# Seven products in place of eight for the second pair of chunks in each feed-forward of a decoder trunk

## The chip, the core and the metric

The kernel runs on one core of a Trainium2 chip. The core has four engines that compute and that run their own instruction queues side by side: TensorE (PE; its weight loads are listed as PEld), VectorE (DVE), ScalarE (ACT) and GpSimd (POOL). SyncE (SP) only issues transfers. TensorE multiplies a stationary tile, which is loaded first, with a moving tile, and writes into PSUM, which has eight banks of 128 partitions x 512 float32; everything else lives in SBUF. Transfers (DMA) run on 16 engines that all queues share: SP's queue loads weights, POOL's queue carries the transfers that add what they bring to what lies at the destination.

The metric is the device time of one execution in microseconds (us), as a median over runs.

## The reference

Two layers, each of them a feed-forward, a mixer and another feed-forward, with a residual and a layer norm behind each of the six. 512 tokens, D_MODEL = 1024, D_FF = 2816, all in float32:

```python
def layer_norm(x, g, b):
    mu = jnp.mean(x, axis=-1, keepdims=True)
    var = jnp.mean(jnp.square(x - mu), axis=-1, keepdims=True)
    return (x - mu) * lax.rsqrt(var + LN_EPS) * g + b

def swiglu_ffn(x, w_gu, w_down):           # w_gu 1024 x 5632, w_down 2816 x 1024
    a, u = jnp.split(x @ w_gu, 2, axis=-1)
    return (jax.nn.silu(a) * u) @ w_down

for l in range(2):
    x = layer_norm(alpha * x + 0.5 * swiglu_ffn(x, ffn1_w_gu[l], ffn1_w_down[l]), ln1_g[l], ln1_b[l])
    x = layer_norm(alpha * x + hybrid_mixer(x, ...), ln2_g[l], ln2_b[l])
    x = layer_norm(alpha * x + 0.5 * swiglu_ffn(x, ffn2_w_gu[l], ffn2_w_down[l]), ln3_g[l], ln3_b[l])
```

The mixer (windowed attention and retention between two projections) is not touched by the change. What follows is about `x @ w_gu`, the up and gate product, in the four feed-forwards; they are called the first to the fourth, in order of time.

## The kernel before, in words

*Precision.* A float32 operand is held as two tiles of a reduced type: the high part is a rounding copy on ScalarE (L173), the low part is the difference between the operand and its high part, on DVE (L174). Such a pair is made by `split`. A product of two operands is three matmuls that add up in PSUM (`mm3`: high x high L188, high x low L189, low x high L190). The names are xh and xl for the activations, transposed, uh and ul for a weight unit of 128 x 1024, Th and Tl for combinations of the activations, raw for the weights as they come from memory.

*The layer's input.* The norm leaves each tile of 128 tokens in Y. Four transposes on TensorE (L488) fill one bank; the split then makes xh and xl from that bank, 512 columns at a time, two banks to a tile of tokens. Tokens 0 to 255 are there before the feed-forward's first matmul; the transposes of tokens 256 to 511 are put into the middle of its opening (`self.finish(self.pend[2:])`), on the schedule of the program text: it is the program's order that decides, and the scheduler keeps matmuls in that order.

*Pairs.* The 5632 columns of `w_gu` are taken in 11 pairs of chunks: a block of 256 columns of a and the 256 columns of u that belong to it. A pair is computed in one of two ways.

- Plain (pairs 0 and 1): four weight units (two of a, two of u), each multiplied with all tokens. For pair 0 the tokens are taken in two halves, so that the work on tokens 0 to 255 goes on while the others are not there yet; one product of pair 1 is drawn forward behind each half of pair 0.
- Strassen's form in the variant of Winograd (pairs 2 to 10, the list `SEVEN`): for a and for u seven half-sized products in place of eight, so 14 products of 12 matmuls of 256 columns. `seven_items` prepares seven weight units: two of them plain blocks, one made of the two lower right blocks, four from sums of blocks (S, at L321, L322, L325, L326, on DVE). `glu7` multiplies. In it the first four products need plain blocks of xh and xl for tokens 0 to 255 only; the others need combinations of the activations T1 to T4 or the block for tokens 256 to 511. The partial results are copied out of PSUM into Q and added to there on DVE. For the combinations, `sums_of_x` first rebuilds x = xh + xl in four additions on DVE (L556), into the part of hT that is written last, and then makes four differences (L560), each split into Th and Tl.

hT is the result of the pair, silu(a) x u x 0.5, written at L631 by DVE (or by the gate of a plain pair).

*The short row of repeated matmuls.* Before the first Strassen pair four matmuls run whose result is thrown away (`lead`, L460: the bank is started afresh by the next matmul).

*Weights.* `Weights` hands out units in the order of its items. It looks LOOK = 6 units ahead, at most UBUFS = 6 units and two raw buffers of 1 MB are in use, and a load is issued (SP's queue, L181) when a raw buffer comes free. The sums, the casts and the low parts of the coming units stand on DVE and ScalarE between the work on results.

*The down projection* at the end of each feed-forward uses the same form; there POOL's queue adds weight blocks from memory onto R (L394).

*Tasks.* `spawn` gives a generator a time in steps; `step`, called after each product, runs those that are due, and `finish` runs the rest.

Of the kernel before, what the change touches and what calls it, by code (L numbers as in the profile page):

```python
# [7 lines left out]
F32 = mybir.dt.float32  # L8
# [25 lines left out]
SEVEN = (2, 3, 4, 5, 6, 7, 8, 9, 10)  # L34
# [65 lines left out]
class Trunk:  # L100
    def __init__(self, tc, ctx):
# [6 lines left out]
        self.pace = None  # L108
        self.halves = 2
# [238 lines left out]
    def ffn_items(self, gu, down, key):  # L348
        items = []
        for fp in range(NFP):  # L350
            a = self.cols_item(gu, fp * 256, (key, "a", fp))
            u = self.cols_item(gu, DFF + fp * 256, (key, "u", fp))
            if fp == 0:
                items += [a[0], u[0], a[1], u[1]]
            else:
                items += self.seven_items(a, u) if fp in SEVEN else a + u
# [99 lines left out]
    def lead(self, out, u):  # L456

        for _ in range(4):
# [23 lines left out]
    def to_xT(self, src, t, c0, dst=None):  # L482
# [8 lines left out]
        self.split(xh[:, c0 : c0 + 4, ts], xl[:, c0 : c0 + 4, ts], bv)  # L491

    def y_to_xT(self, t):
        self.to_xT(self.Y[:, t, :512], t, 0)
        self.to_xT(self.Y[:, t, 512:], t, 4)
# [40 lines left out]
    def ffn(self, g_, b, out=None):  # L536
        nc, tc, W = self.nc, self.tc, self.W
        with ExitStack() as ctx:
# [8 lines left out]

            def sums_of_x():

                x = hT[:, NF - KC :, :]  # L550
                B = [[x[:, i * H : (i + 1) * H, j * 256 : (j + 1) * 256] for j in range(2)] for i in range(2)]
# [26 lines left out]
            def glu7(fp):  # L578
# [4 lines left out]
                for m in range(2):  # L583
# [4 lines left out]
                    if fp == SEVEN[0] and m == 0:  # L588
# [6 lines left out]
                    nc.vector.tensor_add(Q[m][:, 0], Q[m][:, 0], B[m][:, :256])  # L595
                us = W.get()
                u22 = W.get()
                for m in range(2):
                    C.append(self.ps())
                    u = W.get() if m else us  # L600
                    product(A[m], u, 1, T2, False)
                    nc.scalar.copy(Q[m][:, 1], A[m][:, :256])
                    product(C[m], u, 0, T1)
# [599 lines left out]
```

## Time and profile before

| | |
|---|---|
| median of 3 runs | 1752.91 us (1752.52 to 1752.96) |
| the profiled execution | 1752.16 us, with a span of 1750.4 us in the trace |
| granted TensorE clock, mean | 0.999 |
| busy: PE, DVE, ACT, POOL | 1739.2, 1415.5, 927.6, 182.7 us |

An instruction's row gives its start in us, its duration, its engine, its line in the kernel, the operation with result <- operands, and in brackets the idle time of its engine ahead of it with what ended it. "128x1024" is partitions x elements. In a view of windows, "x113" behind a busy time is a number of instructions, and PEclk is the granted clock as a share of full speed. In the queues' view a transfer's row is followed by the time from issue to landing. In the chain of waits a name with q, as PEq, is an engine's sequencer.

### The profile page before, as it was taken

What the parts mean: (1) busy time and instruction counts of PE and PEld (TensorE: products, weight loads), DVE (VectorE), ACT (ScalarE), POOL (GpSimd) and SP (SyncE); (2) the same over time, 40 slices, a digit from 0 to 9 for tenths busy, and PEclk for the clock granted to TensorE, in tenths of its full rate; (3) what the DMA queues carried; (4) which work ended last, traced back from release to release, by engine and by line L of the source; (5) the groups of instructions that cost most, each with busy time, mean ns of one, the idle gap of its engine ahead of it and who ended that gap; (6) DMA issues with size and microseconds to landing.
All of it is one profiled execution on the core that took longest, in us unless ns stands there. A gap on an engine that the chain in (4) does not pass through costs nothing.

```text
span 1750.4 us, 29200 instructions
## 1 busy us (share of the span) xinstructions
PE 1739.2 (99%) x11946; PEld 1580.1 (90%) x11946; DVE 1415.5 (81%) x1975; ACT 927.6 (53%) x1456; POOL 182.7 (10%) x154
## 2 busy tenths in 40 slices
PE   9999999999999999999999999999999999999998
PEld 9999988887789999998899999889877899999886
DVE  7888888856757889879898988988567587988887
ACT  5455656378712455555435556554785234555551
POOL 0000032111111000014000000312011110000231
PEclk9999999999999999999999999999999999999999
DMA  6234389323222243279423334982233123334891
GB/s 193 97 108 134 126 214 220 98 86 95 73 74 73 74 141 101 97 219 217 130 67 109 115 97 157 219 190 91 92 89 97 49 91 103 98 98 144 209 212 48
DMA packets 163765, 216.34 MB, mean 124 GB/s; under 512 B 5168, under 2 KB 116528, under 8 KB 163632
## 3 DMA queue, kind: packets, MB, share of 16 engines
q1 hardware_dynamic: 141872, 172.55, 30.5%
q0 software_dynamic: 21760, 41.95, 13.2%
q8 instruction: 93, 1.52, 0.4%
q14 instruction: 40, 0.33, 0.1%
HBM read 212.38 MB, written 2.10 MB: 123 GB/s over the span
## 4 chain that ended last, share of the span: by engine, by line
PE 48%; DVE 2%; DMA 0%; issue 0%; ACT 0%; POOLq 0%; DVEq 0%; ACTq 0%
PE ps L188 15%; PE ps L189 15%; PE ps L190 15%; PE ps L488 0%; DMA raw<-in_ffn_w_gu_dram 0%; PE ps L1030 0%; PE ps L995 0%; PE ps L1082 0%; PE ps L1022 0%; DVE Y L522 0%; PE ps L1044 0%; DVE ul L174 0%; DVE st L515 0%; DVE Y L513 0%; DVE xl L174 0%; DVE Y L525 0%
## 5 line engine op out<-in xcount | busy, mean ns | idle before, releaser
L188 PE MATMUL ps<-xh,uh 128*128 128x256 f32 (+1 forms) x1616 | 476.0, 295 | 0.0
L189 PE MATMUL ps<-xl,uh 128*128 128x256 f32 (+1 forms) x1616 | 473.0, 293 | 0.5 <-DVE xl L174 0.4
L190 PE MATMUL ps<-xh,ul 128*128 128x256 f32 (+1 forms) x1616 | 473.1, 293 | 0.4 <-DVE ul L174 0.4
L173 ACT CAST uh<-raw 128x1024 fp32r<-128x1024 f32 (+1 forms) x274 | 236.6, 884 | 233.3 <-PE ps L189 127.7
L174 DVE TENSOR_TENSOR ul<-raw,uh 128x1024 fp32r<-128x1024 f32 (+1 forms) x274 | 273.6, 1014 | 56.8 <-ACT uh L173 56.4
L188 PE MATMUL ps<-Th,uh 128*128 128x256 f32 x1152 | 318.0, 276 | 0.0
L189 PE MATMUL ps<-Tl,uh 128*128 128x256 f32 x1152 | 318.0, 276 | 0.0
L190 PE MATMUL ps<-Th,ul 128*128 128x256 f32 x1152 | 318.0, 276 | 0.0
L188 PEld LDWEIGHTS ps<-xh,uh 128*128 128x128 f32 x1616 | 304.1, 188 | 10.5 <-issue 1.6
L190 PEld LDWEIGHTS ps<-xh,ul 128*128 128x128 f32 x1616 | 303.5, 188 | 10.3 <-DVE ul L174 0.8
L189 PEld LDWEIGHTS ps<-xl,uh 128*128 128x128 f32 x1616 | 304.3, 188 | 9.1 <-DVE xl L174 0.9
L188 PE MATMUL ps<-uh,xh 128*128 128x512 f32 x720 | 285.2, 396 | 0.5 <-ACT xh L173 0.5
L189 PE MATMUL ps<-ul,xh 128*128 128x512 f32 x720 | 282.6, 392 | 0.0
L190 PE MATMUL ps<-uh,xl 128*128 128x512 f32 x720 | 281.0, 390 | 0.0
L173 ACT CAST uh<-S 128x1024 fp32r<-128x1024 f32 x144 | 151.3, 1051 | 144.0 <-PE ps L189 140.3
L189 PEld LDWEIGHTS ps<-Tl,uh 128*128 128x128 f32 x1152 | 216.3, 188 | 0.0
L188 PEld LDWEIGHTS ps<-Th,uh 128*128 128x128 f32 x1152 | 216.2, 188 | 0.0
L190 PEld LDWEIGHTS ps<-Th,ul 128*128 128x128 f32 x1152 | 216.2, 188 | 0.0
L174 DVE TENSOR_TENSOR ul<-S,uh 128x1024 fp32r<-128x1024 f32 x144 | 176.0, 1222 | 48.9 <-ACT uh L173 48.4
L394 POOL DMA_DIRECT2D R<-in_ffn_w_down_dram x80 | 97.1, 1217 | 999.8 <-DVE ul L174 912.3
L174 DVE TENSOR_TENSOR ul<-R,uh 128x1024 fp32r<-128x1024 f32 x120 | 145.5, 1223 | 31.5 <-ACT uh L173 31.2
L173 ACT CAST uh<-R 128x1024 fp32r<-128x1024 f32 x120 | 124.8, 1047 | 75.1 <-DMA R<-in_ffn_w_down_dram 36.4
(147 smaller groups left out, 2379.9 us busy)
## 6 DMA issues: line engine op xcount, KB each, us to landing
raw<-in_ffn_w_gu_dram SPq DMA_DIRECT2D x86, 1024.0 KB, 5.3
R<-in_ffn_w_down_dram POOLq DMA_DIRECT2D x80, 512.0 KB, 7.9
raw<-in_w_in_dram SPq DMA_DIRECT2D x18, 1024.0 KB, 5.2
R<-in_ffn_w_down_dram SPq DMA_DIRECT2D x16, 1024.0 KB, 6.2
raw<-in_ffn_w_down_dram SPq DMA_DIRECT2D x12, 1024.0 KB, 7.2
R<-in_ffn_w_down_dram SPq DMA_DIRECT2D x8, 512.0 KB, 4.2
raw<-in_w_in_dram SPq DMA_DIRECT2D x8, 512.0 KB, 5.9
raw<-in_w_out_dram SPq DMA_DIRECT2D x8, 512.0 KB, 6.1
```

Source lines behind the costliest of these rows:

```text
L173: a = self.nc.scalar.copy(hi, src)
L174: b = self.low = self.nc.vector.tensor_sub(lo, src, hi.bitcast(F32))
L188: keep(mm(out, ah, bh, start=start, stop=False, **kw))
L189: keep(mm(out, ah, bl, start=False, stop=False, **kw))
L190: keep(mm(out, al, bh, start=False, stop=stop, **kw))
L394: self.nc.gpsimd.dma_start(src, rows(i, j, g * 2, 2), accum_op=ALU.add))
```

## The change

Pair 1 joins the list `SEVEN`, so that only pair 0 is plain. To make room for that ahead of the transposes, `glu7` becomes a generator that pauses after its first four products:

- the two halves of pair 0 are now: tokens 0 to 255 of both chunks; the first four products of pair 1; the transposes of tokens 256 to 511; tokens 256 to 511 of both chunks of pair 0; the other ten products of pair 1;
- x for the differences is no longer made by the four DVE additions. For tokens 0 to 255 `whole` copies xh with ScalarE into hT, two copies, and POOL's queue then adds xl onto each copy with a transfer of 512 KB (128 partitions x 4 x 256 float32) from SBUF to SBUF. For tokens 256 to 511 ScalarE copies each of the four PSUM banks with the transposed tokens into hT;
- the four differences are made in another order with one more region of hT (`spare`), so that T2 does not overwrite what T1 left;
- in the second part of `glu7`, T1's product comes before T2's, for all pairs;
- the repeated matmuls (`lead`) are eight in place of four, ahead of pair 2, which is the second Strassen pair now;
- a gate's intermediate moves to the tile tag s21, 256 columns wide.

```diff
-SEVEN = (2, 3, 4, 5, 6, 7, 8, 9, 10)
+SEVEN = (1, 2, 3, 4, 5, 6, 7, 8, 9, 10)
...
     def lead(self, out, u):
-        for _ in range(4):
+        for _ in range(8):
...
     def y_to_xT(self, t):
-        self.to_xT(self.Y[:, t, :512], t, 0)
-        self.to_xT(self.Y[:, t, 512:], t, 4)
+        banks = [self.to_xT(self.Y[:, t, c0 * P : c0 * P + 512], t, c0) for c0 in (0, 4)]
+        if self.full is not None:
+            for c0, bv in zip((0, 4), banks):
+                self.nc.scalar.copy(self.full[:, c0 : c0 + 4, t * P : (t + 1) * P], bv)
...
+            x = hT[:, NF - KC :, :]
+            B = [[x[:, i * H : (i + 1) * H, j * 256 : (j + 1) * 256] for j in range(2)] for i in range(2)]
+            spare = hT[:, NF - KC - H : NF - KC, :256]
+
+            def whole(i):
+                ks = slice(i * H, (i + 1) * H)
+                nc.scalar.copy(B[i][0], self.xh[:, ks, :256].bitcast(F32))
+                nc.gpsimd.dma_start(B[i][0], self.xl[:, ks, :256].bitcast(F32), accum_op=ALU.add)
+
             def sums_of_x():
-                for i in range(2):
-                    ks = slice(i * H, (i + 1) * H)
-                    for j in range(2):
-                        ts = slice(j * 256, (j + 1) * 256)
-                        nc.vector.tensor_add(B[i][j], self.xh[:, ks, ts].bitcast(F32), self.xl[:, ks, ts].bitcast(F32))
-                        yield 1
-                for i, (dst, p_, q_) in enumerate(((B[0][0], B[0][1], B[0][0]), (B[0][1], B[1][1], B[0][1]),
-                                                   (B[1][1], B[1][1], B[0][0]), (B[1][0], B[1][0], B[1][1]))):
-                    nc.vector.tensor_sub(dst, p_, q_)
-                    self.split(Th[:, i], Tl[:, i], dst)
-                    yield 1
+                nc.vector.tensor_sub(B[0][0], B[0][1], B[0][0])
+                self.split(Th[:, 0], Tl[:, 0], B[0][0])
+                nc.vector.tensor_sub(spare, B[1][1], B[0][0])
+                self.split(Th[:, 2], Tl[:, 2], spare)
+                yield 1
+                nc.vector.tensor_sub(B[0][1], B[1][1], B[0][1])
+                self.split(Th[:, 1], Tl[:, 1], B[0][1])
+                yield 2
+                nc.vector.tensor_sub(B[1][0], B[1][0], spare)
+                self.split(Th[:, 3], Tl[:, 3], B[1][0])
+                yield 1
...
                     nc.vector.tensor_add(Q[m][:, 0], Q[m][:, 0], B[m][:, :256])
+                yield
                 us = W.get()
...
+            self.full, self.got = x, set()
+            for i in range(2):
+                whole(i)
+            for c in range(2):
+                glu(au[c], c, 0, 256)
+            ahead = glu7(1)
+            next(ahead)
+            self.finish(self.pend[2:])
...
+            xs = self.spawn(sums_of_x(), 0)
+            self.run(xs)
+            for c in range(2):
+                glu(au[c], c, 256, SEQ)
+                W.done(2)
+            self.finish([xs])
+            for _ in ahead:
+                pass
+            for fp in range(2, NFP):
```

Three places show how the instructions move. A row's line numbers are those of its own kernel; those of the changed one are up to six higher or lower (L190 becomes L191, L488 becomes L486, L174 becomes L175, L321 to L326 become L322 to L327).

First, TensorE in the first feed-forward, round the transposes of tokens 256 to 511. Before (ps_34 belongs to the product of pair 1 that was drawn forward; uh_25 is the unit for ps_40, a later product on tokens 0 to 255; xh_87 and xl_88 are xh and xl):

```order
L190 MATMUL ps_34_240<-xh_87,ul_23_171 128x256
L488 MATMUL ps_36_292<-ident_77,Y_89 128x128 x4
L488 MATMUL ps_37_299<-ident_77,Y_89 128x128 x4
L488 MATMUL ps_38_306<-ident_77,Y_89 128x128 x4
L488 MATMUL ps_39_313<-ident_77,Y_89 128x128 x4
L188 MATMUL ps_40_320<-xh_87,uh_25_176 128x256
L189 MATMUL ps_40_320<-xl_88,uh_25_176 128x256
L190 MATMUL ps_40_320<-xh_87,ul_26_177 128x256
```

And after (uh_7 is the first unit of pair 0, now with tokens 256 to 511):

```order
L191 MATMUL ps_43_335<-xh_87,ul_28_181 128x256
L486 MATMUL ps_47_369<-ident_77,Y_89 128x128 x4
L486 MATMUL ps_48_376<-ident_77,Y_89 128x128 x4
L486 MATMUL ps_49_385<-ident_77,Y_89 128x128 x4
L486 MATMUL ps_50_392<-ident_77,Y_89 128x128 x4
L189 MATMUL ps_51_407<-xh_87,uh_7_126 128x256
L190 MATMUL ps_51_407<-xl_88,uh_7_126 128x256
L191 MATMUL ps_51_407<-xh_87,ul_8_127 128x256
```

The matmuls on tokens 0 to 255 that followed the transposes are gone from there; the next matmul reads the tokens just transposed.

Second, DVE in the second feed-forward, where the last differences of x and the results of the first Strassen pair stand among the next pair's weights. Before (Q and ps are a partial result and its bank, S a sum of weights, hT at L631 the result):

```order
L174 TENSOR_TENSOR Tl_5625<-hT_5623,Th_5624 128x1024
L321 TENSOR_TENSOR S_6078<-raw_5849 128x512
L325 TENSOR_TENSOR S_6078<-raw_5849 128x512
L322 TENSOR_TENSOR S_6078<-S_6078,raw_5849 128x512
L631 SCALAR_TENSOR_TENSOR hT_5623<-ps_5986,Q_6014 128x256
L174 TENSOR_TENSOR ul_6018<-raw_5610,uh_6017 128x512
L174 TENSOR_TENSOR ul_6018<-raw_5849,uh_6017 128x512
L326 TENSOR_TENSOR S_6078<-raw_5849,S_6078 128x512
L174 TENSOR_TENSOR ul_6077<-S_6078,uh_6076 128x1024
```

After (ps_5833 and ps_5873 are the two banks called A in `glu7`, one for a and one for u; ps_6049 is a bank called C):

```order
L620 TENSOR_TENSOR Q_5835<-Q_5835,ps_5833 128x256
L327 TENSOR_TENSOR S_6109<-raw_5870,S_6109 128x512
L322 TENSOR_TENSOR S_6178<-raw_5979 128x512
L175 TENSOR_TENSOR ul_6108<-S_6109,uh_6107 128x1024
L175 TENSOR_TENSOR ul_6144<-raw_5870,uh_6143 128x512
L175 TENSOR_TENSOR ul_6144<-raw_5979,uh_6143 128x512
L624 TENSOR_TENSOR Q_5835<-Q_5835,ps_6049 128x256
L620 TENSOR_TENSOR Q_5875<-Q_5875,ps_5873 128x256
L323 TENSOR_TENSOR S_6178<-S_6178,raw_5979 128x512
```

The additions of partial results now stand in this stretch; the second L620 comes behind two sums and three splits of weights, and the pair's last product writes the bank that it reads.

Third, POOL at the end of the first mixer and the start of the second feed-forward. Before (rs is a norm's factor, gvar one of the mixer's):

```order
L1101 TENSOR_TENSOR gvar_5292<-gvar_5292,mhalf 128x8
L521 TENSOR_TENSOR rs_5386<-mv_5383,mhalf 128x1
L521 TENSOR_TENSOR rs_5476<-mv_5473,mhalf 128x1
L521 TENSOR_TENSOR rs_5551<-mv_5548,mhalf 128x1
L521 TENSOR_TENSOR rs_5586<-mv_5583,mhalf 128x1
```

After:

```order
L1095 TENSOR_TENSOR gvar_5359<-gvar_5359,mhalf 128x8
L523 TENSOR_TENSOR rs_5453<-mv_5450,mhalf 128x1
L523 TENSOR_TENSOR rs_5543<-mv_5540,mhalf 128x1
L557 DMA hT_5688<-xl 128x4x256 x2
L523 TENSOR_TENSOR rs_5618<-mv_5615,mhalf 128x1
L523 TENSOR_TENSOR rs_5653<-mv_5650,mhalf 128x1
```

The two transfers that add xl stand ahead of the factors for the third and the fourth tile of tokens.

More of the change, by code (lines that the diff above doesn't have):

```diff
@@ L108, in __init__ @@
         self.pace = None
+        self.full = None
         self.halves = 2
@@ L352, in ffn_items @@
             u = self.cols_item(gu, DFF + fp * 256, (key, "u", fp))
[L353 to L356, printed above, removed]
+            items += self.seven_items(a, u) if fp in SEVEN else [a[0], u[0], a[1], u[1]]
         tail = []
@@ L587, in glu7 @@
                     u = W.get()
-                    if fp == SEVEN[0] and m == 0:
+                    if fp == SEVEN[1] and m == 0:
                         self.lead(A[m], u)
@@ L600, in glu7 @@
                     u = W.get() if m else us
+                    product(C[m], u, 0, T1)
+                    nc.scalar.copy(Q[m][:, 2], C[m][:, :256])
                     product(A[m], u, 1, T2, False)
                     nc.scalar.copy(Q[m][:, 1], A[m][:, :256])
-                    product(C[m], u, 0, T1)
-                    nc.scalar.copy(Q[m][:, 2], C[m][:, :256])
                     W.done()
@@ L628, in gate @@
             def gate(f, a, u, t0, t1):
[L629 to L632 removed]
+                sa = gp.tile([P, 256], F32, tag="s21", name=self.nm("s21"), bufs=2)
+                nc.scalar.activation(sa, a[:, :256], AF.Silu)
@@ L634, in glu @@
+                nc.vector.scalar_tensor_tensor(out=hT[:, f, t0:t1], in0=u[:, :256], scalar=0.5,
+                                               in1=sa, op0=ALU.mult, op1=ALU.mult)
             def glu(au, f, t0, t1):
                 a, u = self.ps(), self.ps()
[L636 to L637 removed]
+                self.projs(a[:, :256], au[0], t0, t1)
+                self.projs(u[:, :256], au[1], t0, t1)
                 gate(f, a, u, t0, t1)
[L640 to L671 removed]
@@ new lines, in ffn @@
+            us = [W.get() for _ in range(4)]
+            self.pin = False
+            au = [us[0:2], us[2:4]]
+            self.finish(self.pend[:2])
+            self.full, self.got = x, set()
[6 more added lines that the diff above has]
+            self.finish(self.pend[2:])
+            assert self.got == {2, 3}
+            self.full = None
+            self.pend = []
@@ L675, in ffn @@
                     self.split(*(v.rearrange("p g f t -> p (g f) t") for v in hv), hT[:, HALF : HALF + 4, :256])
-                if fp in SEVEN:
-                    self.finish([xs])
-                    glu7(fp)
-                    continue
-                a0, a1, u0 = W.get(), W.get(), W.get()
-                glu((a0, u0), fp * 2, 0, SEQ)
-                W.done(2)
-                u1 = W.get()
-                glu((a1, u1), fp * 2 + 1, 0, SEQ)
-                W.done(2)
+                for _ in glu7(fp):
+                    pass
             gctx.close()
```

42 lines of the change are left out of this document (2 added, 40 removed).

## The prediction

> **What bounds the kernel now.** I read the page first, then the windows of the four feed-forwards' openings, then the time lines of the engines there.
>
> ```profile
> PE 1739.2 (99%) x11946; PEld 1580.1 (90%) x11946; DVE 1415.5 (81%) x1975; ACT 927.6 (53%) x1456; POOL 182.7 (10%) x154
> ...
> PE 48%; DVE 2%; DMA 0%; issue 0%; ACT 0%; POOLq 0%; DVEq 0%; ACTq 0%
> ```
>
> TensorE runs through nearly the whole span, so fewer matmuls should pay, if nothing else is late. Whether something is late has to be read where the change sits. I call *opening* the stretch of a feed-forward from its first matmul to the end of the short row of repeated matmuls (L460). The windows give for each stretch the busy time and, in brackets, the count on PE, PEld, DVE, ACT and POOL, then the granted clock, the DMA engines' share and GB/s:
>
> ```profile
> core 0: us, PE busy (x) PEld busy (x) DVE busy (x) ACT busy (x) POOL busy (x), PEclk, DMA share, GB/s
> 7.70:20.10 12.40, 12.03 (x99) 11.59 (x97) 8.93 (x12) 7.13 (x11) 0.00 (x0) 1.00 1.03 322
> 20.10:21.80 1.70, 1.70 (x19) 1.70 (x17) 0.98 (x1) 1.70 (x3) 0.00 (x0) 1.00 0.74 242
> ...
> 549.00:561.80 12.80, 12.80 (x113) 12.77 (x112) 12.33 (x17) 3.72 (x7) 2.37 (x2) 1.00 0.74 246
> 561.80:584.50 22.70, 22.70 (x195) 22.70 (x194) 22.70 (x27) 10.93 (x15) 0.00 (x0) 1.00 0.15 48
> ...
> 596.20:615.20 19.00, 19.00 (x170) 19.00 (x169) 17.02 (x25) 10.14 (x16) 0.00 (x0) 1.00 0.14 47
> ...
> 549.00:596.20 47.20, 47.20 (x358) 44.99 (x357) 40.16 (x51) 17.80 (x26) 2.37 (x2) 1.00 0.41 134
> 876.40:923.40 47.00, 46.87 (x357) 44.50 (x356) 40.50 (x54) 15.60 (x24) 2.91 (x2) 1.00 0.26 87
> ...
> 7.70:56.10 48.40, 47.66 (x359) 44.79 (x358) 39.94 (x50) 23.83 (x34) 0.00 (x0) 1.00 0.54 173
> ```
>
> Three things. A Strassen pair takes 19.0 us for its 168 matmuls (two of the 170 began before), 0.113 us from one start to the next; the plain stretch behind the transposes takes 22.7 us for 192, 0.118 us, at the same granted clock of 1.00. DVE is busy 40 of 47 us, and through the whole of 561.8 to 584.5: it is the second bound, close behind. And in the first opening the DMA engines have no time left until 20.1 (share 1.03).
>
> **The change, part by part.** *Matmuls.* The second pair had 96 matmuls of 256 columns and 48 of 512, worth 192 of 256. It now has 14 products of 12, 168. So 24 x 0.113 = 2.7 us go. The four more lead matmuls cost:
>
> ```profile
> 595.71 0.64 PE L460 MATMUL ps<-uh 128*128 128x256 f32 x4
> 596.19 0.28 PE L188 MATMUL ps<-xh,uh 128*128 128x256 f32 x1
> ```
>
> four in 0.48 us. The gain on TensorE alone is 2.2 us a feed-forward, 9.0 in all (the spacing, 0.113 or 0.118, moves this by 0.1).
>
> *DVE's work.* Prices are start to start in the second feed-forward:
>
> ```profile
> 579.29 1.22 DVE L174 TENSOR_TENSOR Tl<-hT,Th 128x1024 fp32r<-128x1024 f32 x1
> 580.43 1.22 DVE L174 TENSOR_TENSOR ul<-raw,uh 128x1024 fp32r<-128x1024 f32 x1
> ...
> 591.15 1.23 DVE L174 TENSOR_TENSOR ul<-S,uh 128x1024 fp32r<-128x1024 f32 x1 [2.96 <-ACT uh L173]
> 595.98 0.69 DVE L631 SCALAR_TENSOR_TENSOR hT<-ps,Q 128x512 f32<-128x512 f32 x1 [3.60 <-PE ps L190]
> ...
> 598.07 0.69 DVE L321 TENSOR_TENSOR S<-raw 128x512 f32<-128x512 f32 x1
> 598.68 0.69 DVE L325 TENSOR_TENSOR S<-raw 128x512 f32<-128x512 f32 x1
> ```
>
> 1.14 us for 1024 columns, 0.60 for 512; for 256 I take 0.35, half of it and a little. Removed: four additions that rebuilt x (4.6), four weight splits of the plain pair (4.6), its three gates (1.3). Added: six whole splits (6.8) and two halves (1.2) for the seven units, eight sums of weights (4.8), six additions of partial results (2.1), three last products (1.3). The four differences of x stay. Net +5.7 us. DVE idles 47.20 - 40.16 = 7.0 us in the second opening, most of it in the two waits shown, late in it. Afterwards 1.3 us is left, so the opening cannot shrink by more than about 1.3 us, not 2.2, in the second and fourth feed-forward. What turns DVE's lateness into a TensorE wait is the order shown above: the addition that reads the second accumulator (L620) stands behind sums and splits of the next pair, and the last product writes that accumulator. I take -1.3 each; the ends are -2.2 (DVE idles nowhere that matters) and 0.
>
> *ScalarE's copies.* Six more for x, of the kind that take 1.05 us or half of that, on an engine that is busy 18 of 47 us: nothing, except where a weight cast waits behind one; that is under 1 us and inside the range.
>
> *Transposes without a filler.* Before, the 16 transposes of the second half were followed by 24 matmuls on the first half, as these rows of the first and third feed-forward show:
>
> ```profile
> 20.10 1.91 PE L488 MATMUL ps<-ident,Y 128*128 128x128 f32 x16
> ...
> 23.43 2.48 DVE L174 TENSOR_TENSOR xl<-ps,xh 128x512 fp32r<-128x512 f32 x4
> ...
> 887.71 1.91 PE L488 MATMUL ps<-ident,Y 128*128 128x128 f32 x16
> 889.37 0.36 PE L188 MATMUL ps<-xh,uh 128*128 128x256 f32 x1
> ...
> 892.28 0.28 PE L188 MATMUL ps<-xh,uh 128*128 128x256 f32 x1
> 892.69 0.39 PE L189 MATMUL ps<-xl,uh 128*128 128x256 f32 x1
> ```
>
> Now the first matmul behind them reads the new tokens, so TensorE waits out what of the four splits (2.48 us on DVE) lies behind the last transpose: I take 2.3 us, between 1.5 (DVE free, started at the first bank) and 3.3 (the distance from 889.4 to the wait at 892.7 that the third feed-forward has now). The third: -2.2 + 2.3 - 0.3 (its wait now) = -0.2. In the second and fourth the transposes fall earlier, between matmuls that do not need them.
>
> *The first feed-forward's weights.* The second pair's weights arrive here:
>
> ```profile
> 13.27 1.05 ACT L173 CAST uh<-raw 128x1024 fp32r<-128x1024 f32 x1 [0.72 <-DMA raw<-in_ffn_w_gu_dram]
> ...
> 19.74 2.00 ACT L173 CAST uh<-raw 128x1024 fp32r<-128x1024 f32 x2 [1.89 <-DMA raw<-in_ffn_w_gu_dram]
> ...
> L181 SPq DMA_DIRECT2D raw<-in_ffn_w_gu_dram x2: 378/378/379, 13.8 to 15.6; - x2
> ...
> DMA to landing us min/median/max: 5.9/6.4/6.9
> ```
>
> a lands at 19.7, u at 15.6 + 6.9 = 22.5. TensorE is through with its plain part at 20.1 and now needs them at once. For a: cast to 20.8, two sums ahead on DVE, low part done at 22.1: a wait of 2.0 and a product to 24.7. For u: four small DVE operations and the split from 22.1, done at 25.5, so a wait of 0.9, product to 28.1, transposes to 29.8, wait to 32.1, 216 matmuls to 56.6, eight lead to 57.5. It was 56.1: +1.4.
>
> *The DMA that adds.* Per feed-forward two transfers of 512 KB go through POOL's queue, and accumulate. The page prices this kind from 80 of them, 2.9 us of all sixteen engines each (13.2% of 1750.4 over 80):
>
> ```profile
> q0 software_dynamic: 21760, 41.95, 13.2%
> ...
> R<-in_ffn_w_down_dram POOLq DMA_DIRECT2D x80, 512.0 KB, 7.9
> ```
>
> Whether they delay a weight load is seen in a load alone (issued at 573.3) against one of the same size among such transfers (277.7), with POOL's issues round the second:
>
> ```profile
> L181 SPq DMA_DIRECT2D raw<-in_ffn_w_gu_dram x1: 368/368/368, 573.3 to 573.3; - x1
> ...
> DMA to landing us min/median/max: 5.2/5.2/5.2
> ...
> L181 SPq DMA_DIRECT2D raw<-in_ffn_w_down_dram x1: 367/367/367, 277.7 to 277.7; - x1
> ...
> DMA to landing us min/median/max: 9.8/9.8/9.8
> ...
> 276.52 1.21 POOL L394 DMA_DIRECT2D R<-in_ffn_w_down_dram x1 [1.32 <-DVE xl L174]
> 279.09 1.20 POOL L394 DMA_DIRECT2D R<-in_ffn_w_down_dram x1 [1.35 <-DVE xl L174]
> ```
>
> So yes, by up to 4.6 us. The Trainium skill says why ("DMA: Bandwidth & Descriptors", Queues, rings and completion order): each DMA engine goes round its queues packet by packet. In the first feed-forward the two copies that the transfers wait for come behind the cast that ends at 14.3, and end near 16.5, so both transfers run beside the two loads that TensorE already waits for; the delay lies between 0 and 5.8, I take 4.0: +5.4 with the 1.4. In the second and fourth, one load of the pair is issued just before the opening, and ScalarE and DVE stop for it already:
>
> ```profile
> 553.62 2.00 ACT L173 CAST uh<-raw 128x1024 fp32r<-128x1024 f32 x2 [6.09 <-DMA raw<-in_ffn_w_gu_dram]
> 554.70 1.23 DVE L174 TENSOR_TENSOR ul<-raw,uh 128x1024 fp32r<-128x1024 f32 x1 [0.47 <-ACT uh L173]
> ```
>
> The norm and the splits of the last tokens queue behind that DVE instruction, so what the load loses the full DVE queue loses: 0 to 4.6, I take 2.5, the middle, since the load overlaps the transfers in part. That makes -1.3 + 2.5 = +1.2 each. In the third, the loads land long before.
>
> Sum: 5.4 + 1.2 - 0.2 + 1.2 = +7.6 on the profiled execution's 1752.16, that is 1759.8; the median, 1752.91, is 0.75 higher, which is less than the sum can tell.
>
> **The rivals.**
>
> 1. *The transfers hide.* Source and destination are both in SBUF, and only two run at a time; if they finish before the loads start moving, 4.0 + 2 x 2.5 fall away: 7.6 - 9.0 = -1.4, 1750.8: no change, not slower. Against it speaks the share of 1.03 and the 9.8 us. The Trainium skill's fit (same page, Anatomy of one DMA) prices such a transfer at 2.0 us and its bytes at 436 GB/s; for 512 KB that would be 3.2 us, an estimate from the page, and the sum would be about 3.4. The trace disagrees for the accumulating kind: 7.9 us.
> 2. *DVE has room.* With the transfers hidden too, and DVE's 7.0 idle us usable to the end, the second to fourth openings win up to 2.2 each: 1.4 - 4.4 - 0.2 = -3.2, with transposes that also hide -5.2: 1747 to 1749. It decides if the additions of partial results come before TensorE asks for them. Against: DVE without a pause from 561.8 to 584.5.
> 3. *The transfers are dearer.* Their rows are 1 KB, those priced above 2 KB; if a packet has a fixed price, it is 5.8 us each, 11.6 for both. Then x is complete late, the differences of x wait, and all DVE work behind them: the ends of the bounds, +7.2, +3.3, +0.8, +3.3 = +14.6, 1766.8 or more.
>
> **How the numbers follow.** The forecast has 0.52, rival 1 has 0.22, rival 2 has 0.14, rival 3 has 0.12. About 3.5 us, 0.2%, is what a measurement of this kernel can tell from no change. Slower by more: 0.46 of the forecast and 0.12, 0.58. Faster by more: 0.14 and 0.02 of rival 1, 0.16. Within: 0.26. The forecast alone spans 1754 to 1765; with rivals 1 and 2 in, and their rare lower ends and the upper end of 3 left out, the range is 1747 to 1766.
>
> **What would show it.** Second to fourth openings: TensorE waits for an addition Q from ps on DVE ahead of the last product (right), or none (rival 2). First opening: two waits at about 20 and 25 us for the casts of weights, the second longer than 1 us if the transfers delay u (right), under 1 us (rival 1). Time from issue to landing of the loads issued at 13.8 to 15.6: over 8 us or still 6 to 7. Time to landing of POOL's transfers from xl: near 8 to 12 us, or 15 and more (rival 3). A PE idle of about 2 us behind the 16 transposes in the first and third. The forecast is wrong if the first opening ends before 58.5, or the second and fourth take under 47 us.

## The result, and the profile after

The changed kernel takes 1768.68 us (median of 4 runs, 1767.19 to 1774.09), against 1752.72 before on the same chip: a ratio of 1.0097, 95% interval 1.0075 to 1.0119. It is slower, as forecast, by 16 us and not by 7.6, and above the predicted range (1747 to 1766). The profiled execution took 1774.09 us, the longest of the four, so a second profile (the first experiment, 1769.58 us) stands beside it.

The windows of the changed kernel over its four openings, and two stretches of nine pairs behind an opening (the columns are those of the prediction):

```profile
8.50:61.60 53.10, 47.91 (x388) 46.17 (x387) 44.17 (x59) 33.09 (x49) 2.76 (x2) 0.97 0.56 153
554.50:605.10 50.60, 45.69 (x385) 44.72 (x384) 44.68 (x61) 24.89 (x39) 3.35 (x3) 1.00 0.43 116
...
885.30:932.60 47.30, 45.67 (x385) 45.20 (x384) 43.17 (x62) 23.52 (x37) 3.35 (x3) 1.00 0.33 85
...
1425.50:1478.70 53.20, 46.75 (x385) 45.75 (x384) 46.30 (x64) 25.49 (x39) 3.35 (x3) 0.97 0.44 119
...
605.10:776.50 171.40, 171.40 (x1514) 171.40 (x1513) 151.49 (x224) 97.94 (x147) 0.00 (x0) 1.00 0.38 122
1478.70:1656.80 178.10, 178.10 (x1513) 178.10 (x1513) 150.63 (x221) 97.48 (x146) 0.00 (x0) 1.00 0.35 115
```

The openings took 48.4, 47.2, 47.0 and 47.2 us; by their exact starts they now take 53.0, 50.7, 47.3 and 53.2 (the windows' bounds are rounded). TensorE was busy through nearly all of them and now idles 1.6 to 6.5 us in each. Three rows show things that the prediction had no term for: a mean clock of 0.97 in the first and the fourth opening, and the last row, where the same matmuls as in the row above take 178.1 instead of 171.4 us, 0.118 us each instead of 0.113, at a clock of 1.00. Between the openings nothing else moved.

What TensorE waits for in the second opening, in the time line of the changed kernel:

```profile
551.17 1.34 POOL L557 DMA_DIRECT2D hT<-xl  x1 [9.63 <-DVE xl L175]
557.93 1.31 POOL L557 DMA_DIRECT2D hT<-xl  x1 [5.43 <-issue]
558.71 1.12 POOL L523 TENSOR_TENSOR rs<-mv,mhalf 128x1 f32<-128x1 f32 x1
...
559.86 1.29 DVE L527 SCALAR_TENSOR_TENSOR Y<-Y,rs,ln 128x1024 f32<-128x1024 f32 x1 [5.09 <-POOL rs L523]
...
561.21 0.44 PE L486 MATMUL ps<-ident,Y 128*128 128x128 f32 x2 [1.14 <-DVE Y L527]
...
602.19 0.42 DVE L620 TENSOR_TENSOR Q<-Q,ps 128x256 f32<-128x256 f32 x1
...
602.66 0.38 PE L189 MATMUL ps<-Th,uh 128*128 128x256 f32 x1 [2.58 <-DVE Q L620]
```

POOL issues the first transfer at 551.2 and the second only at 557.9, and waits in between for nothing that the profile shows. The norm's factor rs stands behind the second on POOL, DVE stands still 5.09 us for it at the beginning of a stretch in which it has no time to lose, the transposes wait for DVE, and 40 us later the last product waits 2.58 us for the late addition. Before the change the same DVE instruction ran without a wait:

```profile
550.02 1.28 DVE L525 SCALAR_TENSOR_TENSOR Y<-Y,rs,ln 128x1024 f32<-128x1024 f32 x1
```

The first opening:

```profile
22.46 0.38 PE L189 MATMUL ps<-xh,uh 128*128 128x256 f32 x1 [1.59 <-ACT uh L174]
...
23.85 0.38 PE L191 MATMUL ps<-xh,ul 128*128 128x256 f32 x1 [0.89 <-DVE ul L175]
...
27.16 1.05 ACT L174 CAST uh<-raw 128x1024 fp32r<-128x1024 f32 x1 [4.75 <-DMA raw<-in_ffn_w_gu_dram]
...
29.52 0.38 PE L191 MATMUL ps<-xh,ul 128*128 128x256 f32 x1 [0.76 <-DVE ul L175]
```

u's load, issued at 15.9, lands at 27.1; before the change it landed at 22.5. TensorE's wait for it is short, 0.76 us. That is in part because it was slow itself meanwhile: from 24.7 to 28.1 us it had half the clock, which costs up to 1.7 us.

### The profile page after: what moved, and what is told of

It is laid out like the page before. It is cut to its first block, busy times and chain, and to the rows that moved or that the text cites. A ratio compares the mean times of both kernels' runs of the same rounds, so it can differ in the third digit from the quotient of the medians.

```text
span 1772.3 us, 29578 instructions
## 1 busy us (share of the span) xinstructions
PE 1743.7 (98%) x12058; PEld 1590.2 (90%) x12058; DVE 1438.5 (81%) x2031; ACT 964.0 (54%) x1516; POOL 190.6 (11%) x162
## 3 DMA queue, kind: packets, MB, share of 16 engines
q0 software_dynamic: 25984, 46.14, 14.8%
## 4 chain that ended last, share of the span: by engine, by line
PE 91%; DVE 4%; DMA 2%; issue 1%; ACT 1%; SPq 0%; POOL 0%; POOLq 0%; DVEq 0%; ACTq 0%
PE ps L189 29%; PE ps L190 28%; PE ps L191 28%; DMA raw<-in_ffn_w_gu_dram 2%; DVE ul L175 1%; PE ps L486 1%; PE ps L1024 1%; PE ps L989 1%; PE ps L1076 1%; PE ps L1016 1%; ACT uh L174 1%; PE ps L1038 1%; PE ps L1072 0%; DVE Tl L175 0%; DVE xl L175 0%
## 5 line engine op out<-in xcount | busy, mean ns | idle before, releaser
L189 PE MATMUL ps<-xh,uh 128*128 128x256 f32 (+1 forms) x1520 | 443.9, 292 | 4.1 <-ACT xh L174 1.7
L191 PE MATMUL ps<-xh,ul 128*128 128x256 f32 (+1 forms) x1520 | 440.7, 290 | 1.9 <-DVE ul L175 1.8
L190 PE MATMUL ps<-xl,uh 128*128 128x256 f32 (+1 forms) x1520 | 440.4, 290 | 1.6 <-DVE xl L175 1.6
L189 PE MATMUL ps<-Th,uh 128*128 128x256 f32 x1280 | 356.0, 278 | 6.9 <-DVE Q L620 5.1
L174 ACT CAST uh<-raw 128x1024 fp32r<-128x1024 f32 (+1 forms) x274 | 233.1, 871 | 236.5 <-PE ps L190 130.8
L191 PE MATMUL ps<-Th,ul 128*128 128x256 f32 x1280 | 355.4, 278 | 0.0
L190 PE MATMUL ps<-Tl,uh 128*128 128x256 f32 x1280 | 355.4, 278 | 0.0
L175 DVE TENSOR_TENSOR ul<-raw,uh 128x1024 fp32r<-128x1024 f32 (+1 forms) x274 | 269.1, 998 | 55.0 <-ACT uh L174 54.0
L191 PEld LDWEIGHTS ps<-xh,ul 128*128 128x128 f32 x1520 | 286.0, 188 | 9.3 <-DVE ul L175 2.8
L190 PEld LDWEIGHTS ps<-xl,uh 128*128 128x128 f32 x1520 | 287.3, 189 | 7.5 <-DVE xl L175 1.9
L190 PE MATMUL ps<-ul,xh 128*128 128x512 f32 x720 | 282.6, 392 | 0.0
L191 PE MATMUL ps<-uh,xl 128*128 128x512 f32 x720 | 280.9, 390 | 0.0
L189 PEld LDWEIGHTS ps<-Th,uh 128*128 128x128 f32 x1280 | 241.8, 189 | 7.9 <-DVE Q L620 5.5
L190 PEld LDWEIGHTS ps<-Tl,uh 128*128 128x128 f32 x1280 | 240.7, 188 | 0.0
L191 PEld LDWEIGHTS ps<-Th,ul 128*128 128x128 f32 x1280 | 240.7, 188 | 0.0
L174 ACT CAST uh<-S 128x1024 fp32r<-128x1024 f32 x160 | 167.9, 1051 | 131.3 <-PE ps L190 107.9
L175 DVE TENSOR_TENSOR ul<-S,uh 128x1024 fp32r<-128x1024 f32 x160 | 195.3, 1222 | 38.6 <-ACT uh L174 38.5
L175 DVE TENSOR_TENSOR ul<-R,uh 128x1024 fp32r<-128x1024 f32 x120 | 145.3, 1221 | 30.4 <-ACT uh L174 30.2
L174 ACT CAST uh<-R 128x1024 fp32r<-128x1024 f32 x120 | 124.6, 1047 | 74.6 <-DMA R<-in_ffn_w_down_dram 37.5
```

Of the source, the lines that this page charges most:

```text
L174: a = self.nc.scalar.copy(hi, src)
L175: b = self.low = self.nc.vector.tensor_sub(lo, src, hi.bitcast(F32))
L189: keep(mm(out, ah, bh, start=start, stop=False, **kw))
L190: keep(mm(out, ah, bl, start=False, stop=False, **kw))
L191: keep(mm(out, al, bh, start=False, stop=stop, **kw))
```

## The experiments

The theory after the first profile: the transfers carry most of the loss, through POOL's queue in the second and fourth opening and beside SP's loads in the first. Its first rival: DVE has too much to do in the opening, whoever forms x. Its second: the slow spacing behind the fourth opening is the loss. The openings of all kernels (first matmul to the end of the repeated matmuls, in the profiled execution, us), the median, and the ratio with its interval:

| kernel | 1st | 2nd | 3rd | 4th | median | ratio |
|---|---|---|---|---|---|---|
| before | 48.4 | 47.2 | 47.0 | 47.2 | 1752.72 | |
| the change | 53.0 | 50.7 | 47.3 | 53.2 | 1768.68 | 1.0097 (1.0075 to 1.0119) |
| 1 the change again | 54.7 | 51.9 | 46.3 | 54.2 | 1768.65 | 1.0093 (1.0074 to 1.0112) |
| 2 additions on POOL | 51.6 | 49.3 | 48.8 | 47.9 | 1761.09 | 1.0044 (1.0031 to 1.0057) |
| 3 additions on DVE | 52.2 | 46.1 | 47.9 | 46.0 | 1753.75 | 1.0005 (0.9997 to 1.0014) |
| 4 four transfers | 53.6 | 48.3 | 46.3 | 47.9 | 1760.77 | 1.0062 (1.0036 to 1.0087) |
| 5 as 3, transposes first | 49.0 | 46.0 | 45.1 | 46.0 | 1749.00 | 0.9980 (0.9972 to 0.9989) |
| 6 as 5, four leads | 48.8 | 45.4 | 44.6 | 45.4 | 1761.72 | 1.0058 (1.0045 to 1.0071) |
| 7 as 5, copies only | 50.4 | 45.1 | 45.1 | 45.2 | 1748.38 | 0.9973 (0.9964 to 0.9982) |
| 8 the change, transposes first | 52.0 | 51.6 | 45.1 | 52.7 | 1767.19 | 1.0082 (1.0064 to 1.0100) |
| 9 the change, waits filled | 52.9 | 50.7 | 46.3 | 50.6 | 1762.67 | 1.0054 (1.0041 to 1.0066) |
| 10 as 5, T3 first | 47.7 | 44.9 | 45.1 | 44.9 | 1745.50 | 0.9955 (0.9943 to 0.9968) |
| 11 before, with the transfers | 48.4 | 51.6 | 50.7 | 50.8 | 1763.94 | 1.0056 (1.0042 to 1.0070) |

**1, the change again.** Nothing is edited.

> The changed kernel once more, for a second profile, since the first one's execution (1774.1 us) was the slowest of four (1767.2 to 1769.6 the others). Theory 1 (the transfers that add xl, through POOL's queue, carry the loss): the openings are as in the first profile (first 53 us, second 50 to 51, third 47.3, fourth 50 to 53), and the 180 us behind the fourth run at 0.113 us a matmul again, so 278.7 and not 285.4 us to the end; 1767 to 1770. Theory 2 (the slow spacing of 0.118 us behind the fourth opening is what makes the loss): it is there again, 1773 to 1775.

1768.65 us, 1763.6 to 1775.5 in six runs. Windows of this kernel on its nine pairs behind the fourth opening and on four short stretches:

```profile
1480.90:1658.80 177.90, 177.90 (x1543) 176.79 (x1543) 155.43 (x225) 100.61 (x150) 0.81 (x1) 1.00 0.37 122
22.80:26.20 3.40, 3.40 (x16) 3.40 (x17) 1.47 (x3) 0.00 (x0) 0.00 (x0) 0.50 0.76 130
36.30:39.60 3.30, 3.30 (x18) 3.30 (x18) 3.19 (x3) 1.40 (x2) 0.00 (x0) 0.53 1.09 360
603.30:606.60 3.30, 3.03 (x14) 3.03 (x15) 3.30 (x6) 2.37 (x4) 0.00 (x0) 0.52 0.96 319
1477.00:1480.40 3.40, 3.34 (x16) 3.34 (x17) 3.40 (x7) 2.47 (x4) 0.00 (x0) 0.51 1.00 316
```

The slow spacing is gone (1543 matmuls in 177.9 us where there were 1513), so the 6.7 us behind the fourth opening belong to that one execution and not to the usual loss. The others are usual: four times in this run, behind one or more waits, TensorE has half the clock for about 3.4 us, which costs up to 1.7 us each. The runs of the change spread over 12 us, those of the kernel before over 2.4. The Trainium skill ("TensorE: Matmul & The Clock Gate", Part 1: The HAM clock gate) has half rate after an idle window of about 3.4 us; the length of a slow stretch agrees here, while the waits ahead of it were shorter than that (below, 0.88 and 0.76 us).

**2, the additions on POOL.**

```diff
-                nc.scalar.copy(B[i][0], self.xh[:, ks, :256].bitcast(F32))
-                nc.gpsimd.dma_start(B[i][0], self.xl[:, ks, :256].bitcast(F32), accum_op=ALU.add)
+                nc.gpsimd.tensor_add(B[i][0], self.xh[:, ks, :256].bitcast(F32), self.xl[:, ks, :256].bitcast(F32))
```

> The changed kernel, but x of tokens 0 to 255 is formed by two additions on POOL (128x1024 each, about 2.5 us by the 1.3 us of its 128x512 rows), with no ScalarE copy and no transfer. Theory 1 (the transfers): u's load lands in 6 to 7 us again, first opening 4 us shorter; the norm in the second and fourth waits for POOL about 2 us at most and not 5, so that DVE is in time and the 2.6 us wait for its addition ahead of the last product goes: openings of 46 to 48 us; 1755 to 1760. Rival (DVE has too much work in the opening, whoever forms x): the wait ahead of the last product stays at 2 us or more, second and fourth openings stay over 49.5; 1762 to 1767.

1761.09 us, between the two. u landed at 24.5, 7.5 us from issue, so that part of the theory holds; but the first opening is only 1.4 to 3.1 us shorter than in the two profiles of the change, not 4. And the additions had a price of their own, as the time line of the second opening shows:

```profile
548.09 5.76 POOL L556 TENSOR_TENSOR hT<-xh,xl 128x1024 f32<-128x1024 f32 x2 [8.73 <-DVE xl L175]
...
549.42 2.17 DVE L175 TENSOR_TENSOR ul<-raw,uh 128x1024 fp32r<-128x1024 f32 x1
...
551.58 3.35 DVE L524 SCALAR_TENSOR_TENSOR Y<-Y,mv,ln 128x1024 f32<-128x1024 f32 x1
```

DVE's instructions of 1.2 and 1.3 us take 2.2 and 3.4 while POOL adds. This fits the Trainium skill's rule ("SBUF — State Buffer", Who interferes with whom) that a DVE instruction with two SBUF inputs contends with a POOL instruction that reads SBUF. DVE lost 3 us, and the wait for Q ahead of a late product was 2.2 us: moving work from DVE to POOL took as much from DVE as it gave.

**3, the additions on DVE**, as before the change: `nc.vector.tensor_add` in the place of the two lines.

> The changed kernel, but x of tokens 0 to 255 is formed by two additions on DVE as before the change (2.3 us more on DVE in each opening). Theory 1: no transfer, so the first opening is 4 us shorter; the second and fourth lose the 5 us wait for POOL and pay 2.3 us of DVE: 47.5 to 49 us; 1756 to 1762. Rival (DVE's work decides): DVE is later than with the transfers, the wait ahead of the last product grows to 4 us; 1765 or more.

1753.75 us, no change against the kernel before, and 15 us under the change, a little below what the theory had. The first opening missed: 52.2 us is 0.9 to 2.6 less than in the change, not 4, and u's load, with no transfer beside it, still took 8.4 us from issue (6.9 before the change). The second opening, and a stretch of the third, in windows, and two rows of the time line ahead of that stretch:

```profile
552.80:598.90 46.10, 45.12 (x385) 44.90 (x384) 45.73 (x63) 24.29 (x38) 2.36 (x2) 1.00 0.33 108
...
900.20:903.50 3.30, 3.30 (x16) 3.30 (x17) 2.95 (x4) 2.12 (x4) 0.00 (x0) 0.50 1.06 364
```

```profile
898.88 0.38 PE L189 MATMUL ps<-xh,uh 128*128 128x256 f32 x1 [0.88 <-ACT xh L174]
900.02 0.50 PE L190 MATMUL ps<-xl,uh 128*128 128x256 f32 x1 [0.76 <-DVE xl L175]
```

The rival is out: DVE has 2.3 us more to do than in the change and is earlier. With this, the second and fourth openings win 1.1 and 1.2 us, near the 1.3 that the prediction had for them without transfers. What is left of the loss is in the first (52.2) and third (47.9). In the third it is the wait behind the transposes, in two pieces of 0.88 and 0.76, with half the clock right behind them. In the first it is waits of 1.86 and 0.88 us for the second pair's first unit, with half the clock from the second of them on, and 0.82 and 1.19 behind the transposes.

**4, four transfers** of half the size in the place of two.

```diff
-                nc.gpsimd.dma_start(B[i][0], self.xl[:, ks, :256].bitcast(F32), accum_op=ALU.add)
+                for q in range(0, H, 2):
+                    k0 = i * H + q
+                    nc.gpsimd.dma_start(B[i][0][:, q : q + 2, :], self.xl[:, k0 : k0 + 2, :256].bitcast(F32), accum_op=ALU.add)
```

> The changed kernel with the two transfers of 528 packets cut into four of half the size. In the first profile POOL issued the second transfer only 0.3 us after the first had landed, though it waits for nothing of it. If the queue holds a limited number of packets (three transfers of 272 are seen in flight in the down projection), the first two or three go out at once and the queue is blocked for a shorter time: POOL's wait ahead of the norm's factor goes from 5.4 to 3 us or less, the second and fourth openings win 1 to 3 us; 1762 to 1766. If transfers of this kind go one at a time, each waits for the one before: POOL is blocked 5 us or longer, 1767 to 1772.

POOL's issues in the first feed-forward:

```profile
15.82 3.83 POOL L559 DMA_DIRECT2D hT<-xl  x3 [14.41 <-DVE ul L175]
25.45 1.22 POOL L559 DMA_DIRECT2D hT<-xl  x1 [5.80 <-issue]
```

Three go out at once, the fourth 0.3 us after the first has landed (25.19). A limit on packets in the queue would explain both kernels: three of 272 (816) fit, two of 528 (1056) do not. A limit on bytes would not, since the kernel before has three transfers of 512 KB, 272 packets each, in flight together. In the second opening DVE's wait for the norm's factor falls from 5.09 to 0.71 us and the opening from 50.7 to 48.3 (from 51.9 in the first experiment, where a stretch at half clock lies in it). So the blocked queue costs 2.4 us there. The other 2.2 us over the third experiment stay with the transfers, whose neighbours on SP's queue land in 6.7 and 7.5 us instead of 5.0 to 5.2; DVE waits 1.12 and 1.22 us for the casts behind these loads, 0.37 in the third experiment. The median, 1760.77, lies below what was expected; the intervals' ends allow 1759 to 1768, and one run of five took 1776.27.

**11, the transfers alone.** The kernel before, with the second pair plain, the copies and the transfers in the place of the additions on tokens 0 to 255.

> The kernel before the change, with the second pair plain, in which only x of tokens 0 to 255 is formed by ScalarE's copies and the two transfers through POOL's queue in place of two DVE additions. Theory (the transfers block POOL's queue ahead of the norm's factors and slow the weights' loads, whatever form the second pair has): the norm's DVE instruction waits about 5 us for POOL in the second and fourth feed-forward and TensorE's transposes wait behind it, 1 to 4 us each; in the first u's load lands in 10 to 11 us, 0 to 4 us; 1755 to 1764. Rival (the plain second pair leaves room for it, and only with the Strassen form does it cost): 1751.5 to 1754.

```profile
545.77 1.34 POOL L554 DMA_DIRECT2D hT<-xl  x1 [9.62 <-DVE xl L174]
552.56 1.31 POOL L554 DMA_DIRECT2D hT<-xl  x1 [5.45 <-issue]
...
554.49 1.28 DVE L525 SCALAR_TENSOR_TENSOR Y<-Y,rs,ln 128x1024 f32<-128x1024 f32 x1 [5.11 <-POOL rs L521]
...
555.83 0.44 PE L488 MATMUL ps<-ident,Y 128*128 128x128 f32 x2 [1.16 <-DVE Y L525]
```

1763.94 us: 10 us lost with the second pair plain, by the same chain of POOL, norm and transposes (time line of its second opening). In the first opening it costs nothing although u landed 2.5 us later than before (9.3 us from issue): the plain order does not need u so early. The third pays 3.7 us here (a wait of 2.44 us and half the clock behind it), and about 0 in the change, where the transposes come 48 matmuls later.

**5, the transposes ahead of the first four products**, with the additions on DVE.

```diff
-            ahead = glu7(1)
-            next(ahead)
             self.finish(self.pend[2:])
+            ahead = glu7(1)
+            next(ahead)
```

> The kernel with x of tokens 0 to 255 from DVE (the third experiment), and the transposes of tokens 256 to 511 ahead of the Strassen pair's first four products instead of behind them, so that 48 matmuls on tokens 0 to 255 lie between the transposes and the first matmul that reads the new tokens. Theory (TensorE's waits behind the transposes, about 1.6 us, and the wait for the second pair's weights are what the first and third openings lose, and the half clock that follows such waits in some executions is their consequence): first opening 46 to 48.5 us (52.2 in the third experiment, 48.35 before the change), third 44.8 to 45.5 (47.9; 47.0 before), second and fourth unchanged at 46.0; 1745 to 1748, and the runs lie within 2 us of one another. Rival (DVE is the bound in these openings too, and the waits come back ahead of the last products): third 46.5 or more, 1750 to 1753.

1749.00 us, 1748.62 to 1751.02 in 11 runs: faster than both kernels. The third opening fell by 2.8 us to 45.1, as expected. The first, 49.0, was expected at 46 to 48.5: TensorE still waits 0.26 and 0.86 us for the second pair's low parts, and 1.3 us for Q ahead of the last product. No stretch at half clock.

**8, the same edit on the change itself**, with its transfers.

> The changed kernel with its transfers, and only the transposes moved ahead of the first four products. Theory: the waits behind the transposes go in the first and third opening (third 45 to 46 us instead of 46.3 to 47.3), the first still waits for u's load beside the transfer and the second and fourth keep the POOL block (50 to 54 us): 1763 to 1767. Rival (the stalls feed one another, so that without the first ones the rest fits): under 1758.

1767.19 us. The third opening wins as much as in the fifth (45.1), the second and fourth keep their loss: the two causes are apart. The first, 52.0, is 3.1 us longer than in the fifth, from which only the way in which x is formed sets it apart; a wait of 2.28 us is followed there by 6.8 us at half clock, twice the usual length.

**6, four repeated matmuls in place of eight**, on the fifth.

```diff
-        for _ in range(8):
+        for _ in range(4):
```

> The fifth experiment with four repeated matmuls ahead of pair 2 in place of eight (this part of the change undone). If the eight only cost time: 4 x 0.48 us less, 1.9 us under the fifth experiment. If the four more are what brings the spacing back from 0.118 to 0.113 us when the first Strassen pair has run without a pause at 0.118: one or more feed-forwards stay at 0.118 through their nine pairs, 6.8 us longer each; 5 to 25 us over the fifth experiment.

1761.72 us, 12.7 more than with eight. The nine pairs behind the first and the second opening:

```profile
57.00:228.40 171.40, 171.40 (x1514) 171.40 (x1513) 152.03 (x225) 99.27 (x148) 0.00 (x0) 1.00 0.38 124
595.40:773.50 178.10, 178.10 (x1514) 178.10 (x1513) 152.78 (x225) 99.21 (x148) 0.00 (x0) 1.00 0.36 119
```

The openings themselves get 0.2 to 0.6 us shorter, as the price of 0.48 says. But behind the second and the fourth the spacing stays at 0.118 us through all 1512 matmuls, 6.7 us each; behind the first and third four were enough. With eight, 39 of 40 such stretches in ten profiles ran at 0.113; the one that did not is the fourth of the change's first profile, whose eight ran at half clock (0.21 us each). Eight that ran mostly at half clock in the eighth experiment did bring it back, so that is not the whole reason. Not all of the 40 are evidence: only in about half of them did the matmuls just ahead of the eight run at 0.118, and behind all of these but that one the spacing was 0.113. In the kernel before and in the eleventh experiment, where the pair ahead is plain, four were enough in 8 of 8. What sets the two spacings was not found out.

**7, copies only**, on the fifth: the two additions on tokens 0 to 255 are replaced by ScalarE's copy of xh, so xl is left out there.

> The fifth experiment with the two DVE additions left out: x of tokens 0 to 255 is only its high part, copied by ScalarE, so a part of the computation is missing. It prices what forming x costs at all: if DVE's work decides the second and fourth openings, the 1.0 us wait ahead of the last product shrinks by the 2.3 us that DVE saves, openings of 45 us, 2 us under the fifth experiment in all; if the wait has another cause (the order on DVE), nothing changes.

The second and fourth openings fall by 0.9 and 0.8 us to 45.1 and 45.2, and the wait of 0.8 us ahead of the last product is gone, so it does hang on DVE's work. ScalarE's copies, which stay here, cost nothing that shows. The median gains only 0.6 where 2 were expected, within the spread: in its profile the first opening was longer (50.4) by waits for weights.

**10, both T3 products first** in the first Strassen pair, on the fifth.

```diff
+                if fp == SEVEN[0]:
+                    both = [W.get() for _ in range(2)]
+                    for m in range(2):
+                        product(A[m], both[m], 0, T3, False)
+                        nc.vector.tensor_add(Q[m][:, 2], Q[m][:, 2], A[m][:, :256])
                 for m in range(2):
...
                     product(C[m], u, 1, xb(1, 1), False)
```

> The fifth experiment with both products on T3 of the first Strassen pair ahead of its two products on x's last block, so that DVE's addition that the very last product waits for has 24 matmuls more (2.7 us) to be done in. Theory (the addition is late by its place on DVE, behind splits for the next pair): the waits of 1.3 us in the first and of 0.8 us in the second and fourth opening go; 2 to 3 us less, 1746 to 1747. Rival (DVE's work as a whole is the bound, and the wait moves to the next product or its weights): 1748 to 1749.5.

1745.50 us, 1744.99 to 1746.70 in 5 runs, 8 us faster than the kernel before. Windows of the second and third opening:

```profile
548.30:593.30 45.00, 45.00 (x386) 44.97 (x385) 44.83 (x61) 23.90 (x37) 2.37 (x2) 1.00 0.31 103
873.40:918.60 45.20, 45.20 (x386) 45.16 (x386) 44.76 (x65) 23.51 (x37) 3.52 (x2) 1.00 0.19 63
```

TensorE idles nowhere in them, though DVE is busy 44.8 of 45.0 us. The wait ahead of the last product was one of order: more matmuls between the addition and its use cover it, with the work unchanged. (They are 12 more for that addition, 1.4 us, and not the 24 of the expectation, which counted both products.)

**9, the waits filled** with repeated matmuls, on the change: 16 behind the transposes in the first and third, 22 ahead of the last product in the second and fourth.

> The changed kernel with its transfers and its order, and repeated matmuls (their results are thrown away) put where TensorE waits: 16 behind the transposes in the first and third feed-forward (1.8 us, the waits there are 1.6), 22 ahead of the last product in the second and fourth (2.5 us, the wait there is 2.55). Theory (the half clock of 3 to 4 us follows idle time of TensorE, and is what spreads the runs from 1763.6 to 1775.5): the waits for data stay as long, but no half clock behind these places; 1 to 2 us less in each of the openings in which it fell before, so a median of 1761 to 1766 and no run over 1770. Rival (the half clock is not bound to idle time): 1767 to 1771 and the same spread.

1762.67 us, 1761.6 to 1764.7 in five runs: 6 us less than the change by adding matmuls, and the spread is 3 us and not 12. The only stretch at half clock in its openings lies behind the waits of the first opening that were not filled; the third opening shows no idle time:

```profile
884.20:930.60 46.40, 46.40 (x402) 46.16 (x402) 42.28 (x60) 23.20 (x37) 3.35 (x3) 1.00 0.32 82
...
22.70:26.20 3.50, 3.50 (x19) 3.50 (x18) 1.22 (x4) 0.21 (x1) 0.24 (x1) 0.51 0.62 103
```

So the half clock follows idle time of TensorE. It does not follow every wait: the 2.58 us that end at 602.7 in the change's first profile were followed by none, the same wait in the second profile was. How much of the runs' spread is the half clock itself is open. The granted clock of the six runs of the first experiment lies between 0.995 and 0.998, which is about 5 us of the 12 by an estimate (0.003 of 1768); the slow spacing, 6.7 us in the run of 1774.09, can make up the rest, and the longest runs have no profile.

## Why the prediction missed its size

Its sum was +5.4, +1.2, -0.2 and +1.2 for the four openings. The second profile, the one near the median, has +6.4, +4.8, -0.7 and +7.0; 9.4 of the 9.9 us between the two sums lie in the second and fourth opening; that the first came out near is in part luck, as the third point shows.

- **Matmuls: right.** 2.2 us a feed-forward less. The tenth experiment shows it bare: 47.2 to 44.9.
- **DVE's work: right in the sum, wrong in the reason.** DVE is busy 1438.5 us in the change's profile and 1415.5 before, 23.0 more, where four times 5.7 was forecast. Without transfers the second and fourth win 1.1 and 1.2 where 1.3 was forecast, and the wait stood where it was put, ahead of the last product. But "the opening cannot shrink by more than about 1.3" is refuted: it shrank by 2.2 with 2.3 us more of DVE work than the change has, once the addition had room. A sum of busy times against the idle time of an engine was taken for a bound on the opening, though some of DVE's instructions there serve the next pair and can end later.
- **The DMA that adds: the step that failed.** In the second and fourth opening it looked for the delay in SP's loads and took 2.5 us. Without the transfers these openings are 4.6 and 7.2 us shorter than in the change's first profile (third experiment). One load in each was indeed late (7.6 us from issue instead of 5.0 to 5.3), but the larger part came from POOL: the second transfer could not be issued before the first had landed, and the factor of the norm stood behind it. Four smaller transfers win back 2.4 and 5.3 of the 4.6 and 7.2 (up to 1.7 of the 5.3 is the half clock in that profile's fourth opening). The order shown ahead of the prediction had that row, "L557 DMA x2" ahead of rs; the prediction put no price on it. The third rival used the length of the rows to price the transfers themselves; neither it nor the forecast asked whether POOL can issue the second while the first is under way. The trace of before has at most three such transfers in flight, of 272 packets each by the profile's page (21760 over 80); the page after gives the new ones 528 (25984 - 21760 over 8).

  In the first opening the end agreed (61.6 us where 61.5 was forecast), and u's load landed 4.6 us later than before where 4.0 was forecast, but this was luck. The 4.0 were to lengthen TensorE's wait for u to 4.9 us (0.9 + 4.0); it waited 0.76, which by the prediction's own sign speaks for the first rival (its other sign, a load of over 8 us, was met with 11.2). Without transfers the opening still took 52.2 us where the sum has 49.8 (+1.4): the transfers were worth 0.9 to 2.6 us against the third experiment, 3.1 between the fifth and the eighth, and nothing in the eleventh. Waits of 1.59 and 0.89 us for a's unit, the half clock behind them and the waits behind the transposes made up the rest.
- **Transposes without a filler: oversized, then undersized.** 2.3 us were forecast; the waits are 0.88 and 0.76 in the third, 1.6 together. The half clock behind them, up to 1.7 us in some executions, was no term. Moving the transposes ahead of four products took the waits away (fifth experiment).
- **Lead matmuls: priced, not understood.** Four more do cost 0.48 us. That without them 6.7 us are lost in each of two feed-forwards was not seen, although the trace of before shows both spacings and where one ends.
- **The half clock: missing altogether.** Up to four stretches in a run, up to 1.7 us each, and with them a part of the spread. The trace of before has none inside the work, and no wait of TensorE over 0.4 us there; a change that brings waits of 1.6 us or more within a few microseconds can bring this second price with them.

Of the rivals, the third (transfers dearer by packets) came nearest with 1766.8, and the number of packets fits what was seen, but not by the mechanism that it gave: a transfer alone took 5.4 us, x was in time, and what stood still was POOL's queue. The first (transfers hide) and the second (DVE has room) are what the kernel is without transfers, and then with two changes of order. (The 3.4 us beside the first rival does not come out of the terms that the prediction shows.)

## What to carry to other kernels

Before moving work to another engine's queue, list what stands behind it there and ask what happens if the issue itself blocks; a transfer of the same size in shorter rows is not the same load on a queue. Where an engine looks full, see first whether the instruction that is waited for stands behind work that nobody waits for yet; moving it, or moving its user, was worth more here than the work saved. And a wait of TensorE of more than a microsecond or so should be costed with the half clock that may follow.

## What the runs showed of the hardware that was not expected

- POOL's queue took three transfers of 272 packets at once and held back the fourth (fourth experiment), and held back the second of 528 (the change), until about 0.3 us after the first had landed. While held back POOL ran nothing behind.
- A transfer of 512 KB from SBUF to SBUF that adds took 5.4 us from issue to landing by itself in the change's third opening, and 10.5 beside the loads of the first.
- Stretches of about 3.4 us (6.8 once, in the eighth experiment) at half the granted clock came where TensorE had waited 1.6 us and more in all within 3.4 us, in some executions and not in others. Where the waits were filled there was none, and in the four profiles whose waits stay at 1.5 us or less (fifth, sixth, seventh and tenth experiment) none lies inside the work.
- The same 1512 matmuls ran at 0.1133 or at 0.1178 us each, at a granted clock of 1.00, and kept whichever they had from the first to the last. Where the Strassen pair ahead had run at 0.118 (about half of 40 cases), eight matmuls with one stationary tile brought back the first in all cases but one, four in 2 of 4. Why is open.
- A POOL addition of 128x1024 took 2.9 us, and lengthened the DVE instructions beside it from 1.2 to 2.2 and from 1.3 to 3.4 us (second experiment).
